# Pair 1 of a Strassen-like product is forked too, its partial sums get PSUM tiles of their own, and two weight remainders move to VectorE

## The chip, the cores and the metric

The kernel runs on one core of a Trainium2 chip. Its time is the device time of one execution in microseconds (us); three runs of the kernel before gave 734.92 (the median), 732.24 and 737.24. The five engines are called TensorE (PE), VectorE (DVE), ScalarE (ACT), GpSimd (POOL) and SyncE (SP). Each runs its own instructions in program order, and an instruction that waits for another engine holds up all that stands behind it on its own engine. Transfers (DMAs) are issued by SyncE or GpSimd.

## The reference

One layer of a hybrid decoder trunk: 1024 tokens of width 1024, everything in float32.

```python
h = rmsnorm(x, norm_g) * (1 + scale) + shift              # scale, shift, gate from silu(c) @ mod_w + mod_b
cv, cg, cs, lx, ls = split(h @ w_in)                      # five groups of 1024 columns
v = causal_depthwise_conv(cv * sigmoid(cg), dw_w, dw_b)   # 31 taps
v = silu(layernorm(v, cln_g, cln_b)) @ pw2_w + pw2_b
y_conv = v * silu(cs)
xs = causal_depthwise_conv(lx, sc_w, sc_b)                # 4 taps
hs = linear_scan(a, sqrt(1 - a * a) * (i * xs))           # a, i from xs through two gates per head
y_lru = hs * silu(ls)
x = x + (1 + gate) * (concat(y_conv, y_lru) @ w_out)
return rmsnorm(x, final_g)
```

The change concerns one product in this: the lower half of `w_out` times `y_lru`, a 1024 x 1024 matrix times 1024 channels of 1024 tokens, and the layer norm in front of `pw2_w` that is computed beside it.

## The kernel before

Channels lie on the 128 partitions and tokens along the free dimension, so a block is 128 x 1024 (written T; half of it, 512, is H). Every float32 operand is split into a high and a low part (`whi`, `wlo`; `yh`, `yl`), and a product is three matmuls: high by high, high by low, low by high. The low part of a weight, its remainder, is raw minus high. It is made either by VectorE as a subtraction (`SUB`, recorded at L452), or by `remainder()`: ACT writes minus the high part into `wlo` (L433), and GpSimd issues a DMA that adds the raw weight to it from DRAM (L457). A weight's high part is a cast on ACT (L425).

The order in time is: the products with `w_in`, the two gates and the scan of the lru group, then the four *lru pairs* 0 to 3 (the product above), then four pairs with `pw2_w`, then the other half of `w_out`, then the final norm. While the lru pairs run on TensorE, the other engines finish the 31-tap convolution and its layer norm: the mean (`csum`, `csh`, `csl`, `mean`), the squares (`lnsq`, `lnss`), the broadcast of the norm (`lnbc`).

An lru pair p (`lru_pair`) makes the output blocks 2p and 2p+1 out of the weights 40+2p and 41+2p (the lru weights 0 to 7 are 40 to 47 in the names `raw40`, `whi40`, `wlo40`). Part of the product is done in Strassen's way: seven *quarters*, of six matmuls each, called 1, y, 2, z, 3, s and 4, take sums of weight blocks (`lsh`, `lsl`, loaded from DRAM) and sums of the lru output (`yhs`, `yls`); the rest are plain products, twelve matmuls for each half of a block. A pair has 90 matmuls. Some quarters go into several of the four results (two blocks of two halves), and so there are two ways to share them:

- unforked (pairs 0 and 1): each quarter is added to the results that it belongs to by ACT (L433) or by VectorE (L444) as soon as it is done. The tiles are `lp` and `lx`, of two halves each, and `ly`, of one.
- forked (pairs 2 and 3, `FORKP`): quarter 1 goes into half 0 of `lx`; ACT copies it into half 0 of `lp`. Quarter y goes into half 1 of `lx`; ACT copies it into `lk` in SBUF. Quarter 2 adds to half 0 of `lx`; VectorE writes that plus `lk` into half 1 of `lp`. Then z and plain products add to `lp` half 0; quarter 3 adds to `lx` half 0; VectorE writes that plus `lk` into `lx` half 1; s and plain products add to `lp` half 1, and ACT takes `lp` out as one block of 128x1024; quarter 4 and plain products complete `lx`, and ACT takes it out as well.

The finished blocks (`acc`) go to DRAM (`accd`), where the final half of `w_out` adds to them.

The order on each engine comes from a planner (`Plan`): the code declares operations with a priority, a cost and what they read and write, and the planner lists them, keeping the PSUM and SBUF pools in view. Priorities count stages: a smaller number comes earlier. PSUM has a pool `mm` of three tiles with two halves, and a pool `acc` of two tiles with one half; `raw`, `whi` and `wlo` have two buffers each, which the weights use in turn, so that a weight's load waits for the uses of an earlier one.

Constants that the change touches: `FORKP`, which pairs are forked; `FORKN`, the priority of a fork's copies and sums against its stage; `FEVN`, that of taking results out; `LSN`, how many slots ahead a pair's loads of `lsh` and `lsl` may start; `LRV`, which lru weights have their remainder made by VectorE; `QRES`, which nothing in the program reads.

Of the kernel before, what the change touches and what calls it, by code (L numbers as in the profile page):

```python
# [11 lines left out]
AF = mybir.ActivationFunctionType  # L12
ALU = mybir.AluOpType
# [3 lines left out]
T = 1024  # L17
KT = D // P
H = 512
# [85 lines left out]
FINP = -0.5  # L105
BCLATE = False
BEHIND = 0
FORKP = (2, 3)
FORKN = -1.0
FEVAC = ("ACT", "ACT")  # L110
FEVN = 0.3
QT = {(0, c): ("HW", "X") for c in "y234"}
PLACED = ("big",)
MARGINS = 2.0
LSN = 1
LWBS = (5, 6, 7)
LWG = 0
TERMS = {**{("pw2_0", c): ("HW", "X") for c in "1z"}, **{(f"out_{p}", "1"): ("HX", "W") for p in (0, 1, 2, 3)}, **{(f"pw2_{p}", "1"): ("HX", "W") for p in (1, 2, 3)}}
# [1 line left out]
LLATE = 45  # L120
SLOTT = {46: ("HX", "W"), 47: ("HX", "W")}
FINQ = 0.0
LRV = (3, 4, 5)
QRES = 0
SINGLE = (0,)
AHEAD = 4
IDLE, IDLE0 = 12, 4
# [29 lines left out]
class Buf:  # L157
    def __init__(self, pool, name, dtype, parts):
        self.pool, self.name, self.dtype, self.parts = pool, name, dtype, parts
        self.left, self.tile = 0, None  # L160
        self.read, self.written = {}, {}
        self.banks = None

    def __call__(self):
        return self.tile


class Bank:
    def __init__(self):
        self.read, self.written = {}, {}  # L170


class Op:
# [4 lines left out]
class Plan:  # L178
# [23 lines left out]
    def op(self, eng, cost, emit, prio, r=(), w=(), table=None, after=(), reserve=0,  # L202
           columns=0, lock=False, lag=0.0, moved=0.0, flight=FLIGHT):
        o = Op()
        o.lag, o.moved, o.flight = lag, moved, flight
        o.eng, o.cost, o.emit, o.prio, o.table = eng, cost, emit, prio, table
        o.succ, o.ready, o.seq, o.reserve = [], 0.0, len(self.ops), reserve
        o.columns = columns
        o.lock = not lag and eng == "POOL" or eng == "DVE" and lock
        r, w = list(self.keys(r)), list(self.keys(w))  # L210
        preds = set(after)
        for k in r:
            if k in self.writer:
# [12 lines left out]
        for p in preds:  # L226
            p.succ.append(o)
        o.bufs = list(dict.fromkeys(k[0] for k in r + w if isinstance(k[0], Buf)))
        for b in o.bufs:
            b.left += 1  # L230
        o.psum = [(b, any(k[0] is b for k in w)) for b in o.bufs if b.pool in ("mm", "acc") and not b.banks]
        o.psum += [(k[0].banks[k[1]], k in w) for k in dict.fromkeys(r + w) if isinstance(k[0], Buf) and k[0].banks]
        self.ops.append(o)
        return o

# [145 lines left out]
def hymba_layer(ctx: ExitStack, tc: tile.TileContext, xT, vecs, mod_w, w_first, w_in,  # L381
# [37 lines left out]
    def ACT(prio, out, in_, func, n=T, bias=None, scale=None, accum=None, r=(), w=(),  # L419
            reserve=0, after=()):  # L420
        kw = {}

        def emit():
            if func == "copy":
                act.copy(out(), in_())  # L425
                return
            if bias is not None:
                kw["bias"] = bias
            if scale is not None:
                kw["scale"] = scale  # L430
            if accum is not None:
                kw["accum_out"] = accum
            act.activation(out=out(), in_=in_(), func=func, **kw)  # L433
# [15 lines left out]
    def TT(prio, eng, out, a, b, op, n=T, r=(), w=(), reserve=0, after=()):  # L449
        e = dve if eng == "DVE" else pool  # L450
        return S.op(eng, d_cost(n) if eng == "DVE" else p_cost(n),
                    lambda: e.tensor_tensor(out=out(), in0=a(), in1=b(), op=op), prio, r, w,  # L452
                    reserve=reserve, lock=not in_psum(r), after=after)
# [57 lines left out]
    gs, shift, gate1 = ctile("gs", KT), ctile("shift", KT), ctile("gate1", KT)  # L511
# [60 lines left out]
    def mm_k(prio, ps, s, xh, xl, k, cols, off=0, first=0, final=KT - 1, after=(), group="HXW", end=True):  # L572
        wh, wl = whi[s], wlo[s]
        at = LK.index(k) if s[0] == "lru" else k
        terms = [{"H": (wh, xh), "X": (wh, xl), "W": (wl, xh)}[t] for t in group]

        def emit():
            for i, (lhs, rhs) in enumerate(terms):
                for a, b in cols:
                    pe.matmul(ps()[:, a - off:b - off], k3(lhs)()[:, at, :], rhs[k]()[:, a:b],  # L580
                              start=(k == first and lhs is wh and rhs is xh
                                     and (a - off) % H == 0),
                              stop=(k == final and end and i == len(terms) - 1), skip_group_check=True)
# [22 lines left out]
    def half(b, i):  # L606
        return part(b, i * H, i * H + H)
# [295 lines left out]
    for i, ld in enumerate(LOADS):  # L903
        p = due[ld] = i - 100.0
        k = int(ld[1])
# [499 lines left out]
    def lru_pair(p, n, use, firsts, tiles):  # L1405
# [50 lines left out]
                ops.setdefault(c, o)  # L1456

        if p in FORKP:
            x.banks, p0.banks = [Bank(), Bank()], [Bank(), Bank()]

            def plain(s, ps, h):
                for k in rest:
                    mm_k(n + g, ps, s, yh, yl, k, FULL[h:h + 1], first=-1)

            def both(h, to):
                TT(n + FORKN, "DVE", half(to, 1), half(x, 0), half(kept, 0), ALU.add, H, r=[(x, 0), kept],
                   w=[(to, 1)])

            def out_of(i, ps):
                m = 2 * p + i  # L1470
                if FEVAC[i] == "ACT":
                    ACT(n + FEVN + i, tiles[i], ps, AF.Copy, scale=gate1[:, m:m + 1], r=[ps, ("gate1", m)],
                        w=[tiles[i]])
                else:
                    TS(n + FEVN + i, tiles[i], ps, gate1[:, m:m + 1], None, ALU.mult, r=[ps, ("gate1", m)],
                       w=[tiles[i]], n=T)
            quarter("1", "A11", "B11", x, 0, True)
            ACT(n + FORKN, half(p0, 0), half(x, 0), "copy", H, r=[(x, 0)], w=[(p0, 0)])
            g = 0.1
            quarter("y", "S1", "T1", x, 1, True)  # L1480
            kept = big_buf(f"lk{p}")
            ACT(n + FORKN, half(kept, 0), half(x, 1), "copy", H, r=[(x, 1)], w=[kept])
            g = 0.2
            quarter("2", "S2", "T2", x, 0, False)
            both(0, p0)
            g = 0.3
            quarter("z", "A12", "B21", p0, 0, False)
            plain(s0, p0, 0)
            g = 0.4
            quarter("3", "S3", "T3", x, 0, False)  # L1490
            both(0, x)
            g = 0.5
            quarter("s", "S4", "B22", p0, 1, False)
            plain(s0, p0, 1)
            out_of(0, p0)
            g = 0.6
            quarter("4", "A22", "T4", x, 0, False)
            plain(s1, x, 0)
            g = 0.7
            plain(s1, x, 1)  # L1500
            out_of(1, x)
            return ops["1"], ops["3"]
        for c in LORDERS.get(p, LORDER):
            g += 0.12
# [368 lines left out]
```

## Time and profile before

| | us |
|---|---|
| runs: median (lowest, highest) | 734.92 (732.24, 737.24) |
| the profiled execution | 731.9 |
| its span | 730.1 |
| pair 0 in the span | 470.0 to 493.1 |
| pair 1 | to 513.6 |
| pair 2 | to 540.8 |
| pair 3 | to 563.3, where pw2 starts |
| mean granted clock of TensorE | 0.997 |

The page names a line of the program (L1448 is a quarter's matmul, L580 a plain product's, L425 a cast or copy on ACT, L433 another ACT operation, L444 and L452 VectorE's), an engine, an operation, and out<-in by the program's names. A number in square brackets is the time for which the engine was idle before the instruction, with what ended it. In a table by windows come, behind the window, its length, and the busy time and the instructions of PE, PEld (the weight loads, beside PE), DVE, ACT and POOL, then the granted clock, the share of the DMA engines that was busy, and GB/s. In the changed program the lines of the same code lie some 5 to 7 lower: L1441, L573, L418, L426, L437 and L445.

### The profile page before, as it was taken

The page shows a single profiled execution, that of the slowest core. Times are in us where ns is not written, and L with a number is a line of the kernel's source. Part 1 is how long each engine was busy: PE and PEld are TensorE (multiplying, and loading weights), DVE is VectorE, ACT ScalarE, POOL GpSimd, SP SyncE. Part 2 cuts the span into 40 slices and gives each one's busy share as a digit, 9 for nine tenths or more (in the row PEclk, how much of TensorE's full clock was granted, in tenths as well). Part 3 has the DMA queues.
Part 4 walks back from the last instruction along what each step waited for, and adds up shares of the span by engine and source line. Part 5 has one row for each costly group of instructions (what it writes and reads, how often), then busy time and mean ns, then how long its engine had stood idle before and what let it go on. Part 6 is the DMA issues. An engine that isn't in the chain of part 4 may idle for free.

```text
span 730.1 us, 9057 instructions
## 1 busy us (share of the span) xinstructions
PE 717.0 (98%) x3268; PEld 595.6 (82%) x3268; DVE 619.3 (85%) x851; ACT 481.0 (66%) x618; POOL 170.3 (23%) x172
## 2 busy tenths in 40 slices
PE   9999999999999999999999999999899999999996
PEld 8888888888888888888888888878778888888885
DVE  7999999899699898798499994989498966999647
ACT  7650789566698866947949869827488635746322
POOL 0046334354443320233221120100101101110003
PEclk9999999999999999999999999999999999999998
DMA  8946349949989996799898895876935855775006
GB/s 339 406 172 174 58 119 246 262 101 214 216 196 238 243 231 183 169 236 210 176 226 233 226 179 151 256 191 187 223 58 110 228 139 131 232 187 185 30 14 217
DMA packets 46779, 138.58 MB, mean 190 GB/s; under 512 B 5280, under 2 KB 16544, under 8 KB 46624
## 3 DMA queue, kind: packets, MB, share of 16 engines
q0 software_dynamic: 20016, 53.40, 40.9%
q1 hardware_dynamic: 25712, 83.71, 32.7%
q10 hardware_dynamic: 1008, 0.92, 0.4%
q8 instruction: 25, 0.41, 0.2%
q14 instruction: 18, 0.15, 0.1%
HBM read 79.63 MB, written 22.54 MB: 140 GB/s over the span
## 4 chain that ended last, share of the span: by engine, by line
PE 85%; DVE 6%; ACT 4%; issue 3%; DMA 1%; DVEq 0%; POOLq 0%; ACTq 0%
PE ps L580 43%; PE xout L756 6%; PE xpw L756 6%; PE first L889 5%; PE lx L1448 3%; PE ypw L756 3%; PE lp L580 2%; PE lx L580 2%; PE gate L1309 2%; DVE caccs L444 2%; PE y L726 2%; PE zpw L756 2%; PE zout L756 1%; DMA wlo<-in_w_out_dram 1%; PE lp L1448 1%
## 5 line engine op out<-in xcount | busy, mean ns | idle before, releaser
L580 PE MATMUL ps<-uh,whi 128*128 128x512 f32 x576 | 177.5, 389 | 0.0
L580 PE MATMUL ps<-uh,wlo 128*128 128x512 f32 x576 | 177.3, 389 | 0.0
L580 PE MATMUL ps<-ul,whi 128*128 128x512 f32 x576 | 177.3, 389 | 0.0
L580 PEld LDWEIGHTS ps<-ul,whi 128*128 128x128 f32 x576 | 108.1, 188 | 22.5
L580 PEld LDWEIGHTS ps<-uh,wlo 128*128 128x128 f32 x576 | 108.1, 188 | 22.4
L580 PEld LDWEIGHTS ps<-uh,whi 128*128 128x128 f32 x576 | 108.0, 188 | 22.4
L457 POOL DMA_DIRECT2D es<-cq x45 | 40.2, 899 | 134.2 <-ACT cq L433 85.5
L425 ACT CAST whi<-raw 128x1024 fp32r<-128x1024 f32 (+1 forms) x44 | 44.9, 1026 | 37.4 <-issue 22.3
L452 POOL TENSOR_TENSOR wlo<-raw,whi 128x1024 fp32r<-128x1024 f32 x16 | 40.6, 2547 | 87.4 <-ACT whi L425 87.1
L433 ACT ACT_TABLE_LOAD x44 | 56.5, 1283 | 1.5 <-PEq L1865 0.7
L444 DVE SCALAR_TENSOR_TENSOR cacc<-v,V,cacc 128x511 f32<-128x511 f32 (+14 forms) x75 | 55.6, 741 | 0.4
L444 DVE SCALAR_TENSOR_TENSOR caccs<-v,V,caccs 128x511 f32<-128x511 f32 (+6 forms) x70 | 51.9, 742 | 2.0 <-ACT caccs L433 1.0
L444 DVE SCALAR_TENSOR_TENSOR caccs<-c,wsum,caccs 128x511 f32<-128x511 f32 (+6 forms) x70 | 52.0, 743 | 1.0
L457 POOL DMA_DIRECT2D oo<-co x39 | 37.2, 996 | 45.5 <-ACT co L433 20.4
L433 ACT ACTIVATE cq<-v,V 128x511 f32<-128x511 f32 (+14 forms) x45 | 31.8, 707 | 4.5 <-DVE modw L444 4.5
L452 DVE TENSOR_TENSOR wlo<-raw,whi 128x1024 fp32r<-128x1024 f32 (+1 forms) x23 | 27.4, 1194 | 8.4 <-ACT whi L425 8.4
L444 DVE SCALAR_TENSOR_TENSOR modw<-modw,sc 128x1024 f32<-128x1024 f32 x23 | 31.4, 1369 | 0.2 <-DMA modw<-in_mod_w_dram 0.2
L444 DVE SCALAR_TENSOR_TENSOR xs<-ps,V,xs 128x1023 f32<-128x1023 f32 (+2 forms) x24 | 30.6, 1273 | 0.5 <-ACT xs L433 0.5
L433 ACT ACTIVATE cq<-c,wsum 128x512 f32<-128x512 f32 x42 | 29.7, 711 | 0.0
L433 ACT ACTIVATE co<-v,V 128x510 f32<-128x510 f32 (+12 forms) x39 | 26.6, 706 | 0.0
L433 ACT ACTIVATE finsq<-fin 128x512 f32<-128x512 f32 (+2 forms) x14 | 7.9, 570 | 27.4 <-DVE fin L444 14.4
L452 POOL TENSOR_TENSOR o<-fin,bc 128x256 f32<-128x256 f32 (+1 forms) x8 | 7.8, 999 | 68.0 <-ACT bc L425 62.3
(409 smaller groups left out, 1591.4 us busy)
## 6 DMA issues: line engine op xcount, KB each, us to landing
raw<-in_w_in_dram SPq DMA_DIRECT2D x36, 512.0 KB, 5.8
modw<-in_mod_w_dram SPq DMA_DIRECT2D x24, 512.0 KB, 8.3
scsd<-scs SPq DMA_DIRECT2D x8, 512.0 KB, 4.3
raw<-in_w_out_dram SPq DMA_DIRECT2D x8, 512.0 KB, 3.8
accd<-acc POOLq DMA_DIRECT2D x8, 512.0 KB, 6.6
rawpw<-in_pw_dram SPq DMA_DIRECT2D x8, 512.0 KB, 5.0
scsr<-scsd SPq DMA_DIRECT2D x8, 512.0 KB, 5.8
rawout<-in_w_out_dram SPq DMA_DIRECT2D x8, 512.0 KB, 3.3
```

What stands on the lines that cost most here:

```text
L425: act.copy(out(), in_())
L433: act.activation(out=out(), in_=in_(), func=func, **kw)
L444: dve.scalar_tensor_tensor(out=out(), in0=in0(), scalar=scalar, in1=in1(), op0=op0, op1=op1, accum_out=accum)
L452: lambda: e.tensor_tensor(out=out(), in0=a(), in1=b(), op=op), prio, r, w,
L457: return S.op("POOL", ISSUE, lambda: pool.dma_start(out(), a(), accum_op=ALU.add), prio, r, w, lag=RATE * n / T, after=after, flight=flight)
L580: pe.matmul(ps()[:, a - off:b - off], k3(lhs)()[:, at, :], rhs[k]()[:, a:b], start=(k == first and lhs is wh and rhs is xh and (a - off) % ...
L726: pe.matmul(to(), half(*lhs)()[:, j * P:j * P + P], half(*rhs)()[:, c0:c1], start=a == "S1" and j == 0 and t == 0, stop=j == KT // 2 - 1 a ...
L756: pe.matmul(half(ps, 0)(), half(*lhs)()[:, j * P:j * P + P], half(*rhs)(), start=start and at == 0 and i == 0, stop=at == len(order) - 1 a ...
L889: pe.matmul(ps()[:, a - off:b - off], fw_part(lhs, k, i * P, i * P + P)(), rhs()[:, a:b], start=k == 0 and lhs is wh and rhs is xh, stop=k ...
L1309: pe.matmul(ps()[:, c0:c1], lhs()[:, j, :], rhs()[:, c0:c1], start=st == 0, stop=st == 2)
L1448: pe.matmul(half(ps, h)(), lhs()[:, o:o + P], half(*rhs)(), start=begin and at == 0 and t == 0, stop=at == len(order) - 1 and t == len(ter ...
```

## The change

- Pair 1 is forked as well.
- A forked pair has four tiles: `lx` (half 0), `lw` (a second `mm` tile, half 0), and `lc` and `ld` (of the `acc` pool). Quarter 1's copy goes to `lc`, quarter y to `lw`, the first sum to `ld`, the second to `lw`. The planner's book on halves (`Bank`) is gone.
- Each of the four results leaves on its own, by an ACT operation of 128x512 when it is done.
- The remainders of lru weights 1 and 2 (41 and 42) are made by VectorE, that of weight 3 (43) by a DMA.
- The copies and sums of a fork, the evacuations and the loads of `lsh`, `lsl` get other priorities.

```diff
-FORKP = (2, 3)
-FORKN = -1.0
-FEVAC = ("ACT", "ACT")
-FEVN = 0.3
+FORKP = (1, 2, 3)
+FORKN = -3.0
+FEVD = ()
+FEVN = 0.1
...
-LSN = 1
+LSN = 2
...
-LRV = (3, 4, 5)
-QRES = 0
+LRV = (1, 2, 4, 5)
+QRES = 3
...
         if p in FORKP:
-            x.banks, p0.banks = [Bank(), Bank()], [Bank(), Bank()]
+            y0, y1, x1 = acc_tile(f"lc{p}"), acc_tile(f"ld{p}"), mm_tile(f"lw{p}")
 
             def plain(s, ps, h):
                 for k in rest:
-                    mm_k(n + g, ps, s, yh, yl, k, FULL[h:h + 1], first=-1)
-
-            def both(h, to):
-                TT(n + FORKN, "DVE", half(to, 1), half(x, 0), half(kept, 0), ALU.add, H, r=[(x, 0), kept],
-                   w=[(to, 1)])
-
-            def out_of(i, ps):
...
+                    mm_k(n + g, ps, s, yh, yl, k, FULL[h:h + 1], off=h * H, first=-1)
+
+            def both(to):
+                TT(n + FORKN, "DVE", half(to, 0), half(x, 0), half(kept, 0), ALU.add, H, r=[(x, 0), kept],
+                   w=[(to, 0)])
+
+            def out_of(i, h, ps):
+                m, to = 2 * p + i, half(tiles[i], h)
...
+                    ACT(n + FEVN + g, to, half(ps, 0), AF.Copy, H, scale=gate1[:, m:m + 1],
+                        r=[(ps, 0), ("gate1", m)], w=[(tiles[i], h)])
             quarter("1", "A11", "B11", x, 0, True)
-            ACT(n + FORKN, half(p0, 0), half(x, 0), "copy", H, r=[(x, 0)], w=[(p0, 0)])
+            ACT(n + FORKN, half(y0, 0), half(x, 0), "copy", H, r=[(x, 0)], w=[y0])
             g = 0.1
-            quarter("y", "S1", "T1", x, 1, True)
+            quarter("y", "S1", "T1", x1, 0, True)
             kept = big_buf(f"lk{p}")
-            ACT(n + FORKN, half(kept, 0), half(x, 1), "copy", H, r=[(x, 1)], w=[kept])
+            ACT(n + FORKN, half(kept, 0), half(x1, 0), "copy", H, r=[(x1, 0)], w=[kept])
             g = 0.2
             quarter("2", "S2", "T2", x, 0, False)
-            both(0, p0)
+            both(y1)
             g = 0.3
-            quarter("z", "A12", "B21", p0, 0, False)
-            plain(s0, p0, 0)
+            quarter("z", "A12", "B21", y0, 0, False)
+            plain(s0, y0, 0)
+            out_of(0, 0, y0)
             g = 0.4
             quarter("3", "S3", "T3", x, 0, False)
-            both(0, x)
+            both(x1)
             g = 0.5
-            quarter("s", "S4", "B22", p0, 1, False)
-            plain(s0, p0, 1)
-            out_of(0, p0)
+            quarter("s", "S4", "B22", y1, 0, False)
+            plain(s0, y1, 1)
+            out_of(0, 1, y1)
             g = 0.6
             quarter("4", "A22", "T4", x, 0, False)
             plain(s1, x, 0)
+            out_of(1, 0, x)
             g = 0.7
-            plain(s1, x, 1)
-            out_of(1, x)
+            plain(s1, x1, 1)
+            out_of(1, 1, x1)
             return ops["1"], ops["3"]
```

The order moves on several engines. On VectorE in pair 0, before (`acc_3891` is block 0's result, `caccs` and `c` belong to the convolution):

```order
L444 SCALAR_TENSOR_TENSOR caccs_3358<-v_3058,V,caccs_3358 128x503
L452 TENSOR_TENSOR c_2218<-c_2218,oo_2249 128x511
L444 SCALAR_TENSOR_TENSOR acc_3891<-lp_3863,gate_95,acc_3891 128x512
L444 SCALAR_TENSOR_TENSOR acc_3891<-lx_3855,gate_95,acc_3891 128x512
L444 SCALAR_TENSOR_TENSOR caccs_3358<-v_3058,V,caccs_3358 128x502
```

and with the change (`acc_3885` is the same result, `wlo_3954` is weight 42's remainder):

```order
L437 SCALAR_TENSOR_TENSOR caccs_3358<-v_3058,V,caccs_3358 128x503
L445 TENSOR_TENSOR c_2218<-c_2218,oo_2249 128x511
L437 SCALAR_TENSOR_TENSOR acc_3885<-lp_3863,gate_95,acc_3885 128x512
L445 TENSOR_TENSOR wlo_3954<-raw_3770,whi_3944 128x1024
L437 SCALAR_TENSOR_TENSOR acc_3885<-lx_3855,gate_95,acc_3885 128x512
L437 SCALAR_TENSOR_TENSOR caccs_3358<-v_3058,V,caccs_3358 128x502
```

The subtraction for weight 42 now stands between two updates of block 0. On ACT where pair 0 ends and pair 1 begins, before (`acc_3972` is block 1's result, `whi_3944` and `whi_4022` are the weights 42 and 43):

```order
L425 CAST whi_3944<-raw_3770 128x1024
L433 ACTIVATE wlo_3954<-whi_3944 128x1024
L433 ACTIVATE acc_3972<-ly_3886,gate_95 128x512
L425 CAST csh<-csum 128x1024
L425 CAST whi_4022<-raw_3872 128x768
L433 ACTIVATE acc_3972<-lx_3855,gate_95 128x512
L433 ACTIVATE lnss<-cr_3839 128x1024
```

and with the change (`acc_3968` is block 1, `whi_4019` weight 43, `lx_3983` and `lw_4022` the tiles of pair 1):

```order
L418 CAST whi_3944<-raw_3770 128x1024
L426 ACTIVATE acc_3968<-ly_3882,gate_95 128x512
L418 CAST whi_4019<-raw_3895 128x768
L426 ACTIVATE acc_3968<-lx_3855,gate_95 128x512
L418 COPY lc_4029<-lx_3983 128x512
L418 CAST csh<-csum 128x1024
L418 COPY lk_4043<-lw_4022 128x512
L426 ACTIVATE wlo_4047<-whi_4019 128x768
L426 ACTIVATE lnss<-cr_3839 128x1024
```

Pair 1's two copies stand among the mean's cast and weight 43's preparation, and weight 43's cast comes ahead of block 1's last update. On ACT from pair 1 to pair 2, before:

```order
L433 ACTIVATE lnsq5_4143<-c5_2218 128x1024
L425 CAST whi46_4159<-raw46_4119 128x1024
L433 ACTIVATE wlo46_4166<-whi46_4159 128x1024
L425 CAST whi47_4175<-raw47_4131 128x768
L433 ACTIVATE lnsq6_4183<-c6_2645 128x1024
L433 ACTIVATE acc3_4133<-lx1_4059,gate1_95 128x512
L425 COPY lp2_4193<-lx2_4179 128x512
L433 ACTIVATE wlo47_4200<-whi47_4175 128x768
L425 COPY lk2_4205<-lx2_4179 128x512
L433 ACTIVATE lnsq7_4211<-c7_3093 128x1024
```

and with the change:

```order
L418 CAST whi44_4129<-raw44_3963 128x1024
L426 ACTIVATE acc2_4094<-ld1_4055,gate1_95 128x512
L418 CAST whi46_4139<-raw46_4092 128x1024
L426 ACTIVATE lnsq5_4147<-c5_2218 128x1024
L426 ACTIVATE wlo46_4158<-whi46_4139 128x1024
L426 ACTIVATE acc3_4164<-lx1_3983,gate1_95 128x512
L426 ACTIVATE lnsq6_4174<-c6_2645 128x1024
L426 ACTIVATE acc3_4164<-lw1_4022,gate1_95 128x512
L426 ACTIVATE lnsq7_4191<-c7_3093 128x1024
L418 COPY lc2_4198<-lx2_4180 128x512
L418 COPY lk2_4207<-lw2_4194 128x512
```

The cast of weight 44 comes as late as this, the cast of 47 has gone behind pair 2's copies, and two updates of pair 1's second block stand in front of them.

More of the change, by code (lines that the diff above doesn't have):

```diff
@@ L161, in __init__ @@
         self.read, self.written = {}, {}
-        self.banks = None
     def __call__(self):
         return self.tile
-class Bank:
-    def __init__(self):
-        self.read, self.written = {}, {}
 class Op:
@@ L230, in op @@
             b.left += 1
-        o.psum = [(b, any(k[0] is b for k in w)) for b in o.bufs if b.pool in ("mm", "acc") and not b.banks]
-        o.psum += [(k[0].banks[k[1]], k in w) for k in dict.fromkeys(r + w) if isinstance(k[0], Buf) and k[0].banks]
+        o.psum = [(b, any(k[0] is b for k in w)) for b in o.bufs if b.pool in ("mm", "acc")]
         self.ops.append(o)
@@ L1458, in lru_pair @@
         if p in FORKP:
-            x.banks, p0.banks = [Bank(), Bank()], [Bank(), Bank()]
+            y0, y1, x1 = acc_tile(f"lc{p}"), acc_tile(f"ld{p}"), mm_tile(f"lw{p}")
             def plain(s, ps, h):
                 for k in rest:
-                    mm_k(n + g, ps, s, yh, yl, k, FULL[h:h + 1], first=-1)
-            def both(h, to):
-                TT(n + FORKN, "DVE", half(to, 1), half(x, 0), half(kept, 0), ALU.add, H, r=[(x, 0), kept],
-                   w=[(to, 1)])
-            def out_of(i, ps):
[L1470 to L1473, printed above, removed]
-                else:
-                    TS(n + FEVN + i, tiles[i], ps, gate1[:, m:m + 1], None, ALU.mult, r=[ps, ("gate1", m)],
-                       w=[tiles[i]], n=T)
+                    mm_k(n + g, ps, s, yh, yl, k, FULL[h:h + 1], off=h * H, first=-1)
@@ new lines, in both @@
+            def both(to):
[3 more added lines that the diff above has]
+                m, to = 2 * p + i, half(tiles[i], h)
+                if (i, h) in FEVD:
+                    TS(n + FEVN + g, to, half(ps, 0), gate1[:, m:m + 1], None, ALU.mult, r=[(ps, 0), ("gate1", m)],
+                       w=[(tiles[i], h)], n=H)
+                else:
+                    ACT(n + FEVN + g, to, half(ps, 0), AF.Copy, H, scale=gate1[:, m:m + 1],
+                        r=[(ps, 0), ("gate1", m)], w=[(tiles[i], h)])
```

## The prediction

> **What bounds the kernel now.** I read the page's span, busy shares and chain first.
>
> ```profile
> span 730.1 us, 9057 instructions
> PE 717.0 (98%) x3268; PEld 595.6 (82%) x3268; DVE 619.3 (85%) x851; ACT 481.0 (66%) x618; POOL 170.3 (23%) x172
> PE 85%; DVE 6%; ACT 4%; issue 3%; DMA 1%; DVEq 0%; POOLq 0%; ACTq 0%
> ```
>
> TensorE is busy for 717.0 of 730.1 us and makes 85% of the chain, and the change leaves it as many matmuls as before. So the change can gain only what TensorE idles in the stages that it touches, and it can lose wherever TensorE comes to wait. Next come the waits of TensorE (columns: us in total, times, longest), and then the stages: pair 0, pair 1, pair 2, pair 3, and a stretch of the pw2 stage behind them.
>
> ```profile
> PE ly L580 <- DMA wlo<-in_w_out_dram: 1.5, 1, 1.5
> PE lx L1448 <- ACT lp L425: 1.4, 2, 0.7
> PE token_stats L846 <- DVE ones L502: 1.1, 1, 1.1
> PE finbc L809 <- DVE rs65.7_0_5834 L820: 0.9, 1, 0.9
> PE lp L1448 <- DVE lp L452: 0.9, 1, 0.9
> PE lp L580 <- DVE lp L452: 0.9, 1, 0.9
> PE lx L1448 <- ACT lk L425: 0.7, 1, 0.7
> ```
>
> ```profile
> 470.00:494.00 24.00, 22.50 (x99) 18.31 (x98) 21.39 (x27) 10.42 (x15) 2.61 (x3) 1.00 0.76 193
> 494.00:514.00 20.00, 20.00 (x89) 16.45 (x89) 19.37 (x20) 14.95 (x19) 2.67 (x3) 1.00 0.62 169
> 514.00:541.00 27.00, 24.75 (x122) 20.05 (x121) 16.98 (x20) 16.43 (x19) 2.63 (x3) 1.00 0.69 163
> 541.00:563.50 22.50, 20.98 (x91) 16.74 (x90) 18.82 (x26) 17.47 (x24) 3.51 (x4) 1.00 0.50 86
> 563.50:640.00 76.50, 76.50 (x337) 63.01 (x336) 59.63 (x85) 45.28 (x59) 9.60 (x11) 1.00 0.69 186
> ```
>
> The second number is the window's length and the third is TensorE's busy time. It idles 24.00 − 22.50 = 1.50 us in pair 0, nothing in pair 1, 27.00 − 24.75 = 2.25 in pair 2, and 22.50 − 20.98 = 1.52 in pair 3: 5.27 in all. That is the sum of the five groups on ly, lx and lp, to rounding. Pairs 2 and 3 are the forked ones; pair 1, which is not, has no wait. The last row gives the dense step, 76.50 / 337 = 0.227 us a matmul.
>
> Each wait costs more than its idle time, as TensorE's own rows (start, length, idle before) show.
>
> ```profile
> 483.03 0.50 PE L580 MATMUL ly<-yh,wlo 128*128 128x512 f32 x1 [1.50 <-DMA wlo<-in_w_out_dram]
> 513.58 0.39 PE L1448 MATMUL lx<-yh,whi 128*128 128x512 f32 x1
> 515.40 0.39 PE L1448 MATMUL lx<-yhs,lsl 128*128 128x512 f32 x1
> 516.50 0.50 PE L1448 MATMUL lx<-yhs,lsh 128*128 128x512 f32 x1 [0.71 <-ACT lp L425]
> 516.84 0.40 PE L1448 MATMUL lx<-yls,lsh 128*128 128x512 f32 x1
> 518.83 0.50 PE L1448 MATMUL lx<-yhs,lsh 128*128 128x512 f32 x1 [0.68 <-ACT lk L425]
> 521.35 0.50 PE L1448 MATMUL lp<-yh,whi 128*128 128x512 f32 x1 [0.86 <-DVE lp L452]
> ```
>
> A row lasts 0.39 though steps are 0.227 apart, so the last matmul ahead of a gap drains for 0.16 that still counts as busy; behind the gap the first step is 516.84 − 516.50 = 0.34, or 0.11 too long. A restart therefore costs about 0.27. Six waits (1 + 2 + 1 + 1 + 1 by the groups) make 1.6. **The most that can come back is 5.27 + 1.6 = 6.9 us.**
>
> **The change, part by part.** *Separate tiles.* Pair 2 starts at 513.58 with quarter 1 in one half of lx, six matmuls; three of quarter y, in the other half, follow up to 515.40. The fourth waits at 516.50 for ACT's copy of quarter 1, and the row of that copy (below) starts at 515.88, when those three have ended (515.40 + 0.39 = 515.79). So copy and matmuls wait for one another by tile, though they use different halves. At 518.83 quarter 2 waits in its middle for the copy of y in the same way, and at 521.35 quarter z waits for VectorE's sum into the other half of lp. With a tile for each sum these three go. What is left is real: quarter 2 adds to what the first copy reads, but all of y, 6 × 0.227 = 1.4 us, lies between; quarter 3 has z and the plain products ahead of it, 18 matmuls or 4.1 us, to cover the first sum, and quarter 4 as much for the second.
>
> ```profile
> 515.88 0.57 ACT L425 COPY lp<-lx 128x512 f32<-128x512 f32 x1 [0.92 <-PE lx L1448]
> 516.36 0.85 ACT L433 ACTIVATE wlo<-whi 128x768 fp32r<-128x768 f32 x1
> 520.60 0.70 DVE L452 TENSOR_TENSOR lp<-lx,lk 128x512 f32<-128x512 f32 x1 [3.95 <-PE lp L1448]
> 521.20 1.22 DVE L452 TENSOR_TENSOR lnss<-lnss,lnsq 128x1024 f32<-128x1024 f32 x1
> ```
>
> The copy lasts 0.57 and the sum 0.70, so both fit under their covers if their engine is free. Gone in pairs 2 and 3: 1.4 + 0.7 + 0.9 + 0.9 = 3.9 of waits and 5 × 0.27 = 1.35 of restarts.
>
> *Pair 1 forked.* TensorE gets the same quarters in another order. Its eight updates of results (four by ACT, four by VectorE) become four by ACT, two copies and two sums. VectorE loses two instructions of some 0.7; ACT gains two copies. The trace shows no cost where pair 1 now waits for ACT's copy; it lies between nothing and the 0.7 + 0.27 that pairs 2 and 3 pay now. What stands ahead of that copy on ACT prices it:
>
> ```profile
> 492.25 1.05 ACT L425 CAST csh<-csum 128x1024 fp32r<-128x1024 f32 x1 [5.93 <-DVE csum L452]
> 493.20 0.83 ACT L425 CAST whi<-raw 128x768 fp32r<-128x768 f32 x1
> 493.94 0.68 ACT L433 ACTIVATE acc<-lx,gate 128x512 f32<-128x512 f32 x1
> ```
>
> ACT's cast for weight 43 waits for pair 0's last matmul, as its buffer comes free there; behind it stand pair 0's last result and then the copy lc1: 0.74 (493.94 − 493.20) + 0.68 + 0.57 = 2.0. Three matmuls of quarter 1 and six of y come in that time ahead of quarter 2, 9 × 0.227 = 2.0. Adding a start of about 0.15 (the drain above), the copy is **0.15 late**, near the lower end. In pair 3 two casts of halves and pair 2's last result stand ahead of the copy lc3, which by my walk down ACT's order makes it some 0.25 late; in pair 2 it comes out even. With two restarts: 0.15 + 0.25 + 2 × 0.27 = **0.95 lost**.
>
> *Results by halves.* Four half evacuations of 0.68 replace two whole ones.
>
> ```profile
> 534.84 1.10 ACT L433 ACTIVATE acc<-lp,gate 128x1024 f32<-128x1024 f32 x1
> ```
>
> That is 2.7 for 2.2, 0.5 us more of ACT a forked pair. ACT is busy 16.43 of 27.00 in pair 2 and 17.47 of 22.50 in pair 3, which hides it; without that cover it would lengthen a copy's wait by 0.5.
>
> *Remainders.* Before, weight 41's remainder is a DMA that GpSimd issues:
>
> ```profile
> 473.11 0.87 POOL L457 DMA_DIRECT2D wlo<-in_w_out_dram  x1 [9.75 <-PE lx L1448]
> 494.47 0.95 DVE L452 TENSOR_TENSOR wlo<-raw,whi 128x768 fp32r<-128x768 f32 x1
> 503.51 2.08 DVE L452 TENSOR_TENSOR wlo<-raw,whi 128x1024 fp32r<-128x1024 f32 x2
> 481.27 0.73 DVE L444 SCALAR_TENSOR_TENSOR acc<-lx,gate,acc 128x512 f32<-128x512 f32 x1
> ```
>
> It is issued at 473.11 and TensorE gets it at 483.03: 9.9 us, which is the 1.5 wait. As a subtraction on VectorE it takes 0.95, when its raw weight is there. So 1.5 + 0.27 goes. Weight 42 costs VectorE a 1.1 (2.08 for two, with the larger one of them) in front of the update that frees lx for quarter 3 of pair 0; that update, now at 481.27, has no idle time ahead of it, so the trace shows no slack there. Walking VectorE's new order with these lengths I get it done 0.2 before TensorE asks. So it costs nothing, and without that slack up to 1.1 and a restart. Weight 43 leaves VectorE for a DMA:
>
> ```profile
> raw<-in_w_out_dram SPq DMA_DIRECT2D x6, 512.0 KB, 3.8
> accd<-acc POOLq DMA_DIRECT2D x5, 512.0 KB, 5.4
> rawpw<-in_pw_dram SPq DMA_DIRECT2D x2, 512.0 KB, 11.7
> wlo<-in_w_out_dram POOLq DMA_DIRECT2D x2, 384.0 KB, 10.3
> wlo<-in_w_out_dram POOLq DMA_DIRECT2D x3, 512.0 KB, 5.9
> ```
>
> Its issue stands behind the two result stores of pair 0 on GpSimd and follows ACT at about 495.6. With 5.9 or 10.3 to landing it is there at 501.5 or 505.9; pair 1 needs it at about 505. So it costs between nothing and 0.9; I take **0.2**, nearer the smaller row, as transfers of the next stage are few then. The loads of ls may start one slot earlier and SyncE takes raw 43 later, behind two transfers: their landings (3.8 in the median) all come before use. I put **0.2** on them together with result store 5, for whose landing (5.4) ACT waits in front of an evacuation of pair 3.
>
> **Sum.** 6.9 − 0.95 − 0.4 = 5.5 us gained. The profiled run lasted 731.9 us, span 730.1 and 1.8 around it: 731.9 − 5.5 = 726.4. The median of the runs, 734.92, is 1.0041 of the profiled run, so the change should measure **729.0 us** (0.8% faster). Behind pair 3, TensorE runs without a gap from 563.50 to 640.00, so time won ahead of there is kept as long as VectorE and ACT, which have the pw2 operands to make, keep up: the last operand of pw2's pair 0 is some 0.5 early by my walk, as it is now.
>
> **The rivals.** *A: the waits only change their names.* ACT and VectorE run in their given order, and each copy and each sum stands behind work with waits of its own. If each of three forks still waits once for ACT's copy (0.7 + 0.27) and once for VectorE's sum (0.86 + 0.27), that is 3 × 2.1 = 6.3 against 6.9: 731.3 by the profile, 734.3 by the median. For it: pairs 2 and 3 do so today, and pair 1 had no wait. Against: y and z no longer share a tile with what is copied, and the covers are 1.4 and 4.1.
>
> *B: slower.* On ACT the cast of weight 46 now stands ahead of two updates of pair 1, the LN squares and the copy lc2; and its raw weight is loaded into a buffer that the remainder of 45 frees, whose own load waits for the cast of 43. Two loads in series start at about 492.1; the work that follows them in turn (two casts, the subtraction, two updates, two squares, the copy) takes 8.5 by my walk, so lc2 is ready at 500.6 + L1 + L2, where L is the landing time of each. Quarter 2 of pair 2 wants it at 514.5. At the median 3.8 there are 6 us to spare; with 11.7 each, as the rawpw row shows under load, TensorE stands for 9.5 us and the result is 726.4 + 9.5 = 735.9, or 739 by the median. The sign turns where that wait eats the 5.5, at L1 + L2 = 13.9 + 5.5 = 19.4. For it: the DMA share is 0.62 to 0.76 in these stages, and the median of 11.7 stands in the same window. Against: six loads of this very kind had 3.8.
>
> A longer gap could also bear on the clock. The granted clock is 1.00 in all the rows above, with gaps of up to 1.50. The Trainium skill, "TensorE: Matmul & The Clock Gate", Part 1, says that an idle time of about 3.4 us drops TensorE to half clock, and that it takes as long a busy time to recover; the trace neither has such a gap nor a drop here. By that page rival B would cost an estimated 1.7 us more.
>
> *C: a part does nothing.* VectorE makes 42's remainder late, or 43's DMA comes at 505.9: 1.1 + 0.27 or 0.9 + 0.27. Both together still leave 3.1 of gain, 731.8 by the median; this lies inside the range.
>
> **How the numbers follow.** The forecast (with C) has 0.62: gains of 3 to 6.9, that is 728.0 to 731.9 by the median. Rival A has 0.18, rival B 0.13, and 0.07 is for what I don't see. Runs of one kernel lie between 732.24 and 737.24, 2.7 below and 2.3 above their median. The range is 728.0 less 2.7 to A's 734.3 plus 2.3: **725.3 to 736.6**; B lies beyond. About 1% (7.3 us) is what a measurement of this kernel can tell from no change. The forecast's best end is 1.0% and medians move, so of its 0.62 I give 0.28 to faster by over 1%, and 0.34 to within; A is within (0.18); B is within if its loads are little late, slower otherwise (0.03, 0.10). Of the rest 0.03 is faster, 0.04 slower. **Faster 0.31, same 0.55, slower 0.14.**
>
> **What would show it.** Right: no wait of ly on a wlo DMA, none of lp on VectorE, and waits of lx on ACT below 0.5 each; TensorE's idle time between 470 and the start of pw2 at most 1.5; pw2 starting 5 to 7 us earlier in the span. Wrong: a wait of over 1 us on lx, lw or ld (A or B; a gap at pair 2's quarter 2, with ACT's cast of 46 behind a raw load, is B), or an idle time in pw2's pair 0 that was not there.

## The result, and the profile after

The change measures 725.13 us (724.72 to 725.92, six runs) against 732.62 us for the kernel before (six runs, the three named at the start and three more): a ratio of 0.9886, with a 95% interval of 0.9859 to 0.9913. It is faster by 1.1%. The forecast was 729.0 with a range of 725.3 to 736.6, so the time lies just below the range: the direction was right, the forecast gain too small.

The page of the change, its span, busy times and chain:

```profile
span 723.4 us, 9067 instructions
PE 715.6 (99%) x3268; PEld 596.5 (82%) x3268; DVE 619.5 (86%) x850; ACT 481.6 (67%) x623; POOL 169.3 (23%) x171
PE 99%; DVE 1%; issue 0%; DVEq 0%; ACT 0%
```

The span is 6.7 us shorter, and TensorE's share of the chain has risen from 85% to 99%: almost nothing else is late any more. What TensorE waited for, all of it:

```profile
PE token_stats L839 <- DVE ones L495: 1.1, 1, 1.1
PE finbc L802 <- DVE rs65.7_0_5843 L813: 0.9, 1, 0.9
```

Of the seven groups of before, the five in the lru pairs are gone and no new one has come. The windows, cut near the new ends of pairs 0 to 3 and then in the pw2 stage, say the same (third number against second):

```profile
470.00:491.50 21.50, 21.50 (x97) 17.67 (x96) 21.32 (x28) 7.34 (x10) 0.87 (x1) 1.00 0.64 215
491.50:512.00 20.50, 20.50 (x92) 16.85 (x91) 18.70 (x18) 17.68 (x22) 3.50 (x4) 1.00 0.64 140
512.00:536.00 24.00, 24.00 (x123) 20.28 (x122) 19.06 (x22) 18.34 (x23) 2.62 (x3) 1.00 0.77 191
536.00:556.50 20.50, 20.50 (x92) 16.96 (x91) 16.79 (x23) 17.10 (x24) 3.52 (x4) 1.00 0.57 92
556.50:640.00 83.50, 83.50 (x370) 69.12 (x369) 67.77 (x96) 49.12 (x64) 9.58 (x11) 1.00 0.72 191
```

For the comparisons below I use a **length of the lru stage**: from the first matmul of pair 0 to the first zpw matmul of the pw2 stage. It leaves out what differs from one profiled run to the next ahead of the stage and at the tail. The two ends, of before (two rows) and of the change (two rows), from the timeline and from the groups on the tile zpw (behind the durations stand the first and the last start):

```profile
470.03 0.39 PE L1448 MATMUL lx<-yh,whi 128*128 128x512 f32 x1
L756 PE MATMUL zpw<-vhb,whipw x16: 389/389/389, 566.0 to 630.9; 128*128 128x512 f32 x16
```

```profile
470.59 0.39 PE L1441 MATMUL lx<-yh,whi 128*128 128x512 f32 x1
L749 PE MATMUL zpw<-vhb,whipw x16: 389/389/389, 559.7 to 624.3; 128*128 128x512 f32 x16
```

Before it is 566.0 − 470.0 = 96.0, with the change 559.7 − 470.6 = 89.1: 6.9 us less, which is the whole of what the prediction had put as the most that can come back. From the first zpw to the last it is 64.9 and 64.6: nothing is given back later.

### The profile page after: what moved, and what is told of

The parts are those of the page before. It is cut to its first block, busy times and chain, and to the rows that moved or that the text cites. A ratio compares the mean times of both kernels' runs of the same rounds, so it can differ in the third digit from the quotient of the medians.

```text
span 723.4 us, 9067 instructions
## 1 busy us (share of the span) xinstructions
PE 715.6 (99%) x3268; PEld 596.5 (82%) x3268; DVE 619.5 (86%) x850; ACT 481.6 (67%) x623; POOL 169.3 (23%) x171
## 4 chain that ended last, share of the span: by engine, by line
PE 99%; DVE 1%; issue 0%; DVEq 0%; ACT 0%
PE ps L573 54%; PE xout L749 6%; PE xpw L749 6%; PE first L882 5%; PE lx L1441 3%; PE gate L1302 3%; PE ypw L749 3%; PE y L719 2%; PE lx L573 2%; PE zout L749 2%; PE zpw L749 2%; PE lc L573 1%; PE yout L749 1%; PE lw L573 1%; PE ld L573 1%; PE late L882 1%
## 5 line engine op out<-in xcount | busy, mean ns | idle before, releaser
L437 DVE SCALAR_TENSOR_TENSOR modw<-modw,sc 128x1024 f32<-128x1024 f32 x23 | 29.6, 1289 | 0.0
```

The lines of the kernel that those rows point to most:

```text
L437: dve.scalar_tensor_tensor(out=out(), in0=in0(), scalar=scalar, in1=in1(), op0=op0, op1=op1, accum_out=accum)
```

## The experiments

A new wait is charged with its idle time and a restart of 0.27 us. Every kernel's stage length is read as above.

### Quarter y in a tile of its own

```diff
+            yt = acc_tile(f"lw{p}")
...
-            quarter("y", "S1", "T1", x, 1, True)
+            quarter("y", "S1", "T1", yt, 0, True)
...
-            ACT(n + FORKN, half(kept, 0), half(x, 1), "copy", H, r=[(x, 1)], w=[kept])
+            ACT(n + FORKN, half(kept, 0), half(yt, 0), "copy", H, r=[yt], w=[kept])
```

> The kernel before, but in pairs 2 and 3 quarter y has a tile of its own (of the pool acc) instead of half 1 of lx; nothing else moves in the order. Theory (copy and matmuls wait for one another by tile): the three waits of TensorE for ACT's copies (1.4 + 0.7 us) and three restarts of 0.27 go, the two of 0.9 for VectorE's sum stay; span 730.1 - 2.9 = 727.2. Rival (the copies are late in themselves, whatever the tile): the waits for ACT stay, span 730.

Measured: 729.81 us, ratio 0.9961 (0.9944 to 0.9978). The waits of TensorE in the lru pairs:

```profile
PE ly L580 <- DMA wlo<-in_w_out_dram: 1.7, 1, 1.7
PE lp L580 <- DVE lp L452: 0.9, 1, 0.9
PE lp L1448 <- DVE lp L452: 0.9, 1, 0.9
```

The three waits for ACT are gone, the two for VectorE stay, as the theory had it. The stage is 93.3 us long, 2.7 less than before, and 2.9 less without the 0.2 by which this run's wait for the DMA is longer. On ACT, VectorE and GpSimd the instructions of the stage stand in the same order in both traces, so what is undone here is only that matmuls and a copy used halves of one tile. That these three waits were by tile is shown.

### The remainders alone

```diff
-LRV = (3, 4, 5)
+LRV = (1, 2, 4, 5)
```

> The kernel before with the remainders of weights 41 and 42 on VectorE and that of 43 by a DMA, and nothing else of the change. Theory: the wait of 1.5 for the DMA and one restart go, the five waits of pairs 2 and 3 stay: span 728.3. Rival (VectorE comes late with 42 in pair 0, or 43's DMA is late in pair 1): a new wait of 0.9 to 1.1 and a restart, span 729.5.

Measured: 731.55 us, ratio 0.9985 (0.9971 to 0.9999); the stage is 95.2 us, 0.7 less. The rival was about right in its size (a span of 729.5, measured 729.4), but the new wait is in another place:

```profile
PE lx L1448 <- ACT lp L425: 1.4, 2, 0.7
PE lp L1448 <- DVE lp L452: 0.9, 1, 0.9
PE lp L580 <- DVE lp L452: 0.9, 1, 0.9
PE lx L1448 <- DVE acc L444: 0.8, 1, 0.8
PE lx L1448 <- ACT lk L425: 0.7, 1, 0.7
```

```profile
508.71 0.50 PE L1448 MATMUL lx<-yhs,whi 128*128 128x512 f32 x1 [0.75 <-DVE acc L444]
```

The wait for the DMA is gone, and quarter 4 of the *unforked pair 1* now waits 0.75 for VectorE to take quarter 3 out of lx. TensorE comes there about 1.8 us earlier, VectorE does not (it was busy for 19.37 of 20.00 us in that pair before). 1.5 + 0.27 gained and 0.75 + 0.27 lost is 0.75, which is what the stage shows.

### Own tiles in pairs 2 and 3 alone

The changed program with the constants of before:

```diff
-FORKP = (1, 2, 3)
-FORKN = -3.0
+FORKP = (2, 3)
+FORKN = -1.0
...
-FEVN = 0.1
+FEVN = 0.3
...
-LSN = 2
+LSN = 1
...
-LRV = (1, 2, 4, 5)
+LRV = (3, 4, 5)
```

> The change's forked form (a tile for each sum, results by halves) in pairs 2 and 3 alone, with the remainders, the priorities and the unforked pair 1 of before. Theory: five waits (3.94 us) and five restarts (1.35) go, the wait of 1.5 for the DMA stays: span 730.1 - 5.3 = 724.8. Rival (the new priorities are needed, without them ACT's copies come late): half of it or less, span 727 to 730, with waits on ACT's copies of lc or lk.

Measured: 727.87 us, ratio 0.9935 (0.9913 to 0.9957). In the lru pairs one wait is left:

```profile
PE ly L573 <- DMA wlo<-in_w_out_dram: 1.8, 1, 1.8
```

The stage is 91.2 us, 4.8 less than before, or 5.1 but for the 0.3 by which the DMA came later in this run. The theory said 5.3. So the new form in pairs 2 and 3 brings some three quarters of the change, and the new priorities are not needed for that. Its results leave by halves here too, so the two waits for VectorE's sums go with own tiles and half results together; no run takes these two apart.

### The change with pair 1 unforked

```diff
-FORKP = (1, 2, 3)
+FORKP = (2, 3)
```

> The change, but with pair 1 unforked. Theory: pair 1 had no wait, so its fork brings TensorE nothing: span 723.4 within 0.5. Rival (forking pair 1 frees VectorE, which is what keeps pairs 2 and 3 fed): new waits for VectorE in pairs 2 and 3, span 725 to 727.

Measured: 726.90 us, ratio 0.9916 (0.9890 to 0.9943). The stage is 90.4 us, 1.3 longer than with the change. The two waits in the lru pairs that are new against the change:

```profile
502.82 0.50 PE L1441 MATMUL lx<-yhs,lsh 128*128 128x512 f32 x1 [0.28 <-ACT acc L426]
510.53 0.50 PE L1441 MATMUL lx<-yhs,whi 128*128 128x512 f32 x1 [0.61 <-DVE acc L437]
```

0.28 + 0.61 and two restarts are 1.4. My theory fell: the fork of pair 1 does bring something. The rival's place was wrong too, since pairs 2 and 3 have no wait here. It is pair 1 itself which waits for its own updates as soon as TensorE arrives without the stall in pair 0; the run on the remainders alone shows the same.

### The copy into lc, twice

The order is that of the change, and each of the three copies of quarter 1 is issued twice in a row.

```diff
-            if func == "copy":
-                act.copy(out(), in_())
+            if func in ("copy", "twice"):
+                for _ in range(1 + (func == "twice")):
+                    act.copy(out(), in_())
...
-            ACT(n + FORKN, half(y0, 0), half(x, 0), "copy", H, r=[(x, 0)], w=[y0])
+            ACT(n + FORKN, half(y0, 0), half(x, 0), "twice", H, r=[(x, 0)], w=[y0])
```

> The change, with the copy of quarter 1 into lc issued twice in a row in each of pairs 1 to 3, the order otherwise the same: 0.52 us more of ACT just ahead of quarter 2. In the trace of the change these copies end 0.11, 0.30 and 0.27 before quarter 2's first matmul. Theory (the copies are just in time, and a wait costs its length and a restart of 0.27): waits of about 0.4, 0.2 and 0.25 for lc and three restarts, pw2's first zpw matmul 1.6 us later than with the change (561.3 against 559.7). Rival (the copies have slack that the rows don't show): no wait, 559.7.

Measured: 727.00 us, ratio 0.9920 (0.9905 to 0.9935). The waits, one for each pair:

```profile
494.18 0.50 PE L1442 MATMUL lx<-yhs,lsh 128*128 128x512 f32 x1 [0.39 <-ACT lc L419]
515.98 0.50 PE L1442 MATMUL lx<-yhs,lsh 128*128 128x512 f32 x1 [0.20 <-ACT lc L419]
540.57 0.50 PE L1442 MATMUL lx<-yhs,lsh 128*128 128x512 f32 x1 [0.24 <-ACT lc L419]
```

The expected waits were 0.4, 0.2 and 0.25. The stage is 90.7, 1.6 longer than the change's: 0.83 of waits and three restarts of 0.27 (0.81). So the copies are just in time, with 0.1 to 0.3 to spare, and the price of a restart stands (0.26 each here).

### The old priority of copies and sums

```diff
-FORKN = -3.0
+FORKN = -1.0
```

> The change, with the old priority of a fork's copies and sums (FORKN -1 in place of -3), under which ACT takes weight 43's preparation and the mean's cast ahead of pair 1's copy. Theory: by the lengths of the rows (0.8 and 0.95) that copy ends 1.7 later, and quarter 2 of pair 1 waits 1.6 and a restart: zpw at 561.5. Rival (other work fills in, the priority is of no weight): 559.7.

Measured: 726.54 us, ratio 0.9917 (0.9900 to 0.9934); the stage is 90.2, 1.1 longer than the change's. The planner also moved the mean's matmuls ahead of quarter 2, and it is these that wait:

```profile
494.10 0.74 PE L1543 MATMUL mean<-csh,ones_d 128*128 128x512 f32 x2 [0.96 <-ACT csh L418]
```

0.96 + 0.27 = 1.2. The copy of quarter 1 itself is as late as expected: it runs from 493.95 for 0.59, so it ends 1.6 after the nine matmuls in front of quarter 2 (492.98). The mean's two matmuls fill part of that time. So the priority matters, for less than I expected and by another wait.

### The change with the old remainders

```diff
-LRV = (1, 2, 4, 5)
+LRV = (3, 4, 5)
```

> The change, with the remainders as before: weight 41 by the DMA, 42 too, 43 by VectorE. Theory: the wait of 1.5 to 1.8 for the DMA of 41 is back with its restart, nothing else: zpw at 561.5 to 561.8. Rival (with pair 1 forked the later part has slack in VectorE only as 43 has left it): a wait for VectorE in pair 1 on top, 562.5 or more.

Measured: 728.60 us (727.19, 727.53, 729.68, 729.92), ratio 0.9942 (0.9923 to 0.9960). The wait for the DMA is back and nothing waits for VectorE, so the theory holds on the place; the size is not that of either, since the stage of the profiled execution (729.68) is 92.9 us, 3.8 longer than the change's. The timeline of TensorE behind the wait, and then the windows around it (the number after the busy times is the granted clock):

```profile
484.50 0.50 PE L573 MATMUL ly<-yh,wlo 128*128 128x512 f32 x1 [2.09 <-DMA wlo<-in_w_out_dram]
484.83 0.50 PE L573 MATMUL ly<-yh,whi 128*128 128x512 f32 x1
485.13 0.63 PE L573 MATMUL ly<-yl,whi 128*128 128x512 f32 x1
485.56 0.63 PE L573 MATMUL ly<-yh,wlo 128*128 128x512 f32 x1
...
487.69 0.63 PE L573 MATMUL ly<-yl,whi 128*128 128x512 f32 x1
488.12 0.52 PE L573 MATMUL ly<-yh,wlo 128*128 128x512 f32 x1
488.48 0.39 PE L1441 MATMUL lx<-yhs,lsh 128*128 128x512 f32 x1
```

```profile
480.00:484.00 4.00, 2.41 (x11) 1.67 (x9) 3.96 (x7) 2.11 (x2) 0.59 (x1) 1.00 0.98 265
484.00:488.00 4.00, 3.50 (x9) 2.77 (x10) 2.56 (x4) 0.00 (x0) 0.27 (x1) 0.62 0.96 316
488.00:492.00 4.00, 4.00 (x18) 3.25 (x18) 1.86 (x3) 0.69 (x1) 0.00 (x0) 0.95 0.73 144
```

```profile
485.00:488.00 3.00, 3.00 (x8) 2.31 (x8) 1.59 (x3) 0.00 (x0) 0.00 (x0) 0.50 0.94 291
```

This time the wait was 2.09 us, and behind it seven matmuls go by steps of 0.43 (485.13 to 488.12) in place of 0.227: 1.4 us more. The 0.62 is a mean over 4 us; from 485 to 488 the granted clock is 0.50. 2.09 + 0.27 + 1.4 = 3.8 is what the stage lost. The four runs fall into two pairs: 727.19 and 727.53 at a mean clock of 0.998, 729.68 and 729.92 at 0.995. The lower pair lies 2.1 to 2.4 above the change's median, which is what a wait of 1.8 to 2.1 and a restart would cost without the drop; those two have no trace. This I had not expected, and the two runs that follow are on it.

### The DMA of weight 41, later

To the kernel before, GpSimd gets small subtractions (128x64, into a tile that nothing reads) ahead of its DMA for weight 41: three in one run, seven in the other.

```diff
+        for _ in range(3):                # the second run: 7
+            t = slow()[:, -64:].bitcast(F32)
+            pool.tensor_tensor(out=spare, in0=t, in1=t, op=ALU.subtract)
         pool.dma_start(out(), a(), accum_op=ALU.add)
```

> The kernel before, with three small subtractions into a spare tile on GpSimd (some 0.3 us each) ahead of its DMA for weight 41, so that TensorE's wait in pair 0 grows from 1.5 to about 2.4 us; the order is otherwise the same. In the profile of the change with the old remainders a wait of 2.1 was followed by matmul steps of 0.43 and a granted clock of 0.62 for some 3 us. Theory (a wait of over about 2 us makes the clock drop): clock below 0.8 behind the wait in the profile, times 0.9 + 1.5 = 2.4 above the kernel before's lowest (731.3), 733.7 in most runs. Rival (that drop had nothing to do with the wait): clock 1.00, 732.3.

> As the run before, with seven such subtractions: a wait of about 3.6 to 3.8 us. Theory: the clock drops in every run, 2.2 + 1.5 = 3.7 above the lowest time of the kernel before, 735.0. Rival: clock 1.00, 733.5.

GpSimd's subtractions took longer than the 0.3 that I had put (5.8 us for the three, 8.3 for the seven), so the waits came out longer. With three of them the profiled run waits 3.30 us (the wait, and the windows behind it):

```profile
485.65 0.79 PE L586 MATMUL ly<-yh,wlo 128*128 128x512 f32 x1 [3.30 <-DMA wlo<-in_w_out_dram]
```

```profile
484.00:488.00 4.00, 2.35 (x6) 1.87 (x7) 2.54 (x4) 0.00 (x0) 0.23 (x1) 0.57 0.96 211
488.00:492.00 4.00, 4.00 (x12) 3.14 (x11) 0.00 (x0) 0.69 (x1) 0.00 (x0) 0.58 0.08 15
492.00:496.00 4.00, 4.00 (x19) 3.27 (x19) 3.63 (x5) 0.00 (x0) 0.88 (x1) 1.00 0.00 0
```

That execution lasted 737.28 us. The median of its ten runs is 733.03 (ratio 1.0015, 0.9997 to 1.0032): six runs of 732.15 to 733.09 at a mean clock of 0.996 to 0.998, three of 734.66 to 734.99 at 0.993, and the profiled one at 0.992. So the theory's "in most runs" was wrong, and the drop itself was right in the profiled execution; how long the six short runs waited is not known. The profiled stage is 100.4 us, 4.5 longer than before: 1.8 for the longer wait (3.30 − 1.50) and 2.7 for the slow steps behind it. With seven subtractions the wait is 6.41 us, the granted clock stands at 0.54 and 0.50 in the two windows of 4 us from 484 to 492, and the four runs lie at 739.48 to 740.36: ratio 1.0100 (1.0074 to 1.0127). 4.9 us more of waiting than before (6.41 − 1.5) leaves 2.8 of the 7.7 that it costs (740.18 − 732.50) for the clock and, with it, for slower steps. In the three traces in which this wait was 2.09, 3.30 and 6.41 us, it cost its length, a restart and 1.4 to 2.8 us through a lower clock.

### The loads one slot later

```diff
-LSN = 2
+LSN = 1
```

> The change, with a pair's loads of lsh and lsl starting one slot later, as before (LSN 1): on SyncE the raw weights 45 and 46 then go ahead of pair 2's loads. Theory: the loads land before use either way, zpw at 559.7 within 0.3. Rival: pair 2's quarter y waits for lsh, up to 1.

Measured: 725.41 us (two runs, ratio 0.9899, 0.9879 to 0.9918). The stage is 90.1, 1.0 longer, by one wait of which neither side had thought:

```profile
513.99 0.50 PE L1441 MATMUL lw<-yhs,lsh 128*128 128x512 f32 x1 [0.62 <-ACT acc L426]
```

With the weights 45 and 46 loaded first, ACT prepares the later weights earlier. The cast and the remainder of weight 47 (at 510.27 and 511.58) now stand ahead of block 3's last half, which leaves lw at 513.26 in place of 512.61, and pair 2's quarter y has to wait for that.

## Why the prediction was wrong in size, by its own steps

The signs that the prediction named for being right all came: no wait of ly on a wlo DMA, none of lp on VectorE, no idle time of TensorE in the lru pairs, and the first zpw matmul 6.3 us earlier. What failed is the size, by two terms that are marked below.

*The bound.* "The most that can come back is 6.9 us" was right: the stage is 6.9 shorter. Idle time of 5.27 and a restart for each wait were the right two terms. The doubled copy repeats the 0.27; in the runs with one or two new waits a restart comes out between 0.1 and 0.4, from stages that are read to 0.1.

*Separate tiles.* Right, in mechanism and size. The waits of y and of quarter 2 for ACT went with the tile, as the first experiment shows by itself; those for VectorE's sums went in the run with the new form in pairs 2 and 3 alone. The covers of 1.4 and 4.1 held: nothing waits for a sum.

*Pair 1 forked, 0.95 lost.* This is the first term that failed: no wait came in pair 1 or in pair 3. ACT and TensorE (with the weight load ahead of quarter 2) at the start of pair 1, in the change:

```profile
491.74 0.84 ACT L418 CAST whi<-raw 128x768 fp32r<-128x768 f32 x1 [6.66 <-PE lx L573]
492.48 0.68 ACT L426 ACTIVATE acc<-lx,gate 128x512 f32<-128x512 f32 x1
493.06 0.59 ACT L418 COPY lc<-lx 128x512 f32<-128x512 f32 x1
493.58 1.04 ACT L418 CAST csh<-csum 128x1024 fp32r<-128x1024 f32 x1
```

```profile
491.27 0.39 PE L573 MATMUL lx<-yl,whi 128*128 128x512 f32 x1
491.49 0.39 PE L573 MATMUL lx<-yh,wlo 128*128 128x512 f32 x1
...
493.70 0.19 PEld L1441 LDWEIGHTS lx<-yhs,lsh 128*128 128x128 f32 x1 [0.20 <-ACT lc L418]
493.76 0.44 PE L1441 MATMUL lx<-yhs,lsh 128*128 128x512 f32 x1
494.04 0.40 PE L1441 MATMUL lx<-yls,lsh 128*128 128x512 f32 x1
```

The order is the one that I had walked: cast, result, copy. Two steps of the walk were wrong. The first is where it starts: the prediction let the cast wait for pair 0's last matmul (491.49, whose step ends at 491.72) and 0.15 beyond, that is until 491.87. The cast starts at 491.74. It overwrites `whi`, and the last matmul that reads `whi` is the one before, at 491.27. That the cast waits for that one is inferred: it starts 0.47 behind it, and the copy at 515.88 before the change starts 0.48 behind the matmul that it waits for (515.40). The second is the lengths: I had added those of the rows, 0.74 + 0.68 + 0.57 = 1.99, where cast and result take 493.06 − 491.74 = 1.32 from start to start and the copy 0.59: 1.91. Together the copy ends at 493.65, 0.11 ahead of quarter 2's first matmul (493.76), where I had it 0.15 late; by the prediction's own figures, unrounded, 0.15 + 1.99 − 2.04 is 0.10. There is no slack to speak of: the weight load for quarter 2 did wait 0.20 for the copy, and quarter 2's first step is 0.28 long in place of 0.227, which is all that the fork costs.

In pair 3 the copy that I had 0.25 late ends 0.27 early:

```profile
536.82 0.62 ACT L418 CAST vha<-cr 128x512 fp32r<-128x512 f32 x1 [0.16 <-PE lw L573]
537.34 0.68 ACT L426 ACTIVATE acc<-lw,gate 128x512 f32<-128x512 f32 x1
537.92 0.61 ACT L418 CAST vha<-c 128x512 fp32r<-128x512 f32 x1
538.43 0.59 ACT L418 COPY lc<-lx 128x512 f32<-128x512 f32 x1
```

The four rows add up to 2.50, and from the first start to the copy's end it is 2.20: 0.30 of the 0.52 is again the adding of rows. The rest stays open, as the prediction does not give that walk in numbers. So 0.3 to 0.5 us decided between a wait and none.

The prediction also gave the fork of pair 1 no gain, and that was wrong too: without it 1.3 us goes back to waits in pair 1 for VectorE and ACT. It asked what is late next where the stall on weight 41 goes, and looked at weight 42 in pair 0; it was pair 1's updates, which the fork takes away.

*Results by halves.* Hidden, as said.

*Remainders.* The stall is gone. The update that frees lx for quarter 3 of pair 0 runs from 483.83 for 0.75, and quarter 3 takes lx at 484.87, so 0.29 is left where the prediction had 0.2. Weight 43's DMA, issued at 496.5, landed after 5.2 us, at 501.7, and pair 1 needs it at about 505. The price of the stall can be higher than was put, though: 1.5 and a restart is what it cost in the profile of before, and with 2.09 the lower clock came on top. *Landings, 0.4 lost:* nothing was lost.

*The sum's frame.* This is the second term, and the larger one. In the profiled executions the forecast is 726.4 and the measurement 725.26, 1.1 apart: 0.95 and 0.4 less 0.2. I then took the result to the median by 1.0041, the median of three runs over the profiled one. The product is 729.4; the forecast's 729.0 is 0.4 below it, a slip. Either way the step adds 2.6 to 3.0 us, and it was wrong: twenty later runs of the kernel before have a median of 732.48, 1.0008 of the profiled run, and the change's own median is 0.13 below its profiled run. The same frame set the low end of the range: 728.0 less 2.7 is the lowest of the three runs, 732.24, less 6.9. From the profiled 731.9 the same gain leads to 725.0, outside the range.

Two of the first three runs were high, 737.24 and 734.92. Of the forty runs of before beside the experiments none is above 735.29, and six are above 734.5. Why is not shown. Part of the scatter may go with the stall: the sets of runs that have the wait for weight 41 as it comes (twenty of before, y's tile, the new form in pairs 2 and 3 alone, old remainders) spread over 2.6 to 4.0 us, those without it over 0.7 to 2.2, and the change stays within 724.72 to 725.92. Against it: seven runs of before beside the doubled copy spread over 0.9 only, and the four runs with seven subtractions over 0.9 as well. The mean clocks fit in part: of the six runs above 734.5 three are at 0.993 and three at 0.996, where short ones are found too, and a clock of 0.50 at the very end of a run can lower the mean as well (the profiled run with pair 1 unforked has 0.995 and a clock of 0.50 from 718 on). So a factor that may have held the scatter of a stall was applied to a kernel without the stall; that the high runs of before had the clock drop is not shown, as none of them has a trace.

*The rivals.* A and B did not come about. For B: the cast of weight 46 runs at 507.31 without idle time ahead of it in the change, so its two loads in series were there. C's weight 42 came in time.

## What to carry to other kernels

Where two engines use halves of one tile, look at whether they wait for one another in the middle of a group of instructions: such waits go with a tile of their own, without any change in the order. When walking an engine's order by hand, add the steps from start to start, not the lengths of the rows, and look for the last matmul that reads the buffer, which need not be the last of its group; with slacks of some tenths of a us the difference decides. And a forecast should be compared within profiled runs: a median of three that is above the profiled run may hold scatter that the change does not have.

## What was not expected of the hardware

A wait of 2.09 us was enough for the granted clock to fall to 0.50, while waits of 1.5, 1.7 and 1.8 in the same place left it at 1.00 in their profiles. The last of these, around its wait of 1.82:

```profile
481.00:491.00 10.00, 8.18 (x36) 6.45 (x36) 8.23 (x12) 1.93 (x3) 1.73 (x2) 1.00 0.56 133
```

With 2.09 the clock fell at 485.0, half a us after TensorE had begun again; with 3.30 and 6.41 it fell at 484.5 and 484.3, 2.1 to 2.2 us into the wait. The Trainium skill, "TensorE: Matmul & The Clock Gate", Part 1, puts the idle time that halves the clock at about 3.4 us. All three traces speak against that as a lower bound here. The clock was back 3.9 us after TensorE had begun again in the run with 2.09, near what the page says of the way back, but only after 5.7 and 5.9 us in the two others. What a wait between 1.8 and 2.1 us does, and whether it depends on when it comes, stays open.
